# A decoder block on one core: one gather for both rows of an expert, and the low part of the up-projection's rows on GpSimd

## The chip, the cores and the metric

The kernel runs on one core of a Trainium2 chip. A core has a matrix engine (TensorE, PE in the profile; its weight loads are PEld), a vector engine (VectorE, DVE), a scalar engine (ScalarE, ACT), GpSimd (POOL) and a queue engine that issues DMAs (SyncE, SP). The on-chip memories are SBUF and PSUM; PE writes to PSUM, and DVE and ACT read and write both. The metric is the device time of one execution in microseconds (us).

## The reference, cut to what matters

The block has a mixer (attention and a short convolution), a layer norm, an expert layer and a second norm, for 1024 tokens of width 1024. All is float32. The expert layer has 16384 experts; each expert is one row `u` and one row `v` of 1024 numbers. A token picks 8 heads x 16 = 128 experts with gates `g`, and then:

```
u = jnp.take(u_experts, ec, axis=0)
a = jax.nn.gelu(jnp.einsum('tkd,td->tk', u, xc), approximate=False)
vv = jnp.take(v_experts, ec, axis=0)
return jnp.einsum('tk,tkd->td', gc * a, vv)
...
h = layer_norm(DN_ALPHA * h + ff, ln2_g[l], ln2_b[l])
```

## The kernel before

The 1024 tokens are eight blocks of 128. For four of them (`ROWS`, blocks 0, 1, 6 and 7) the expert layer is computed by **gathered rows**: for each of the 128 picks k, GpSimd gathers the picked row of `u` for all 128 tokens (an indirect DMA of 128 rows of 4 KB, line 148), DVE multiplies it by the token's `h1` and sums it into one number per token (line 150, the "up product"; a second small instruction reads the sum out). After 128 picks ACT applies gelu to all 128 x 128 numbers (line 152), DVE multiplies by the gates (line 153), and then for each pick GpSimd gathers the row of `v` (line 160) and DVE adds row times number to an accumulator in PSUM (line 162, the "down add"). That is 4 x 256 = 1024 operations on DVE and as many gathers. The rows stand in five buffers of 4 KB per partition (tag `t4k`); a gather waits until the operation five back has freed its buffer.

The other four blocks (2 to 5, 512 tokens) go through the **dense** layer: all 16384 experts in 128 chunks, on PE. `up(c)` loads chunk c of the transposed `u` table (`uraw`), splits it into a high part `uh` (a copy on ACT, line 120) and a low part `ul` (a subtraction, line 121), and multiplies both with the split `hT`, 24 matmuls. Then come the gelu `ge` on ACT, its product with the gates `gq` on DVE (line 690), and a split into `Wh` (ACT) and `Wl` (DVE). `down(q, jj)` does the same for four chunks' rows of `v`: `vh` on ACT, `vl` on GpSimd, 24 matmuls on the split W, and two adds of the result to `accT` on DVE (line 722). There are 128 such up units and 128 down units; `uh`, `ul`, `vh` and `vl` have two buffers each, the `W` parts five, and the raw loads four.

**Stage 1**, ahead of the dense stage, runs the mixer, the norm and the picking of experts for two blocks at a time; its last part builds the gates for the dense layer (`oh` and `ol` on DVE, 64 of each). The gathered operations are laid between its steps as soon as a block's picks are known (`step`, `advance_rows`), and further into the dense units by `advance(unit)`. The last part of the program (`finish`) transposes `accT`, adds `h1` and norms the four dense blocks.

The order of the instructions on each engine is set by a scheduler when the kernel is built; each engine runs its own in order.

Of the kernel before, what the change touches and what calls it, by code (L numbers as in the profile page):

```python
# [77 lines left out]
def block_kernel(ctx: ExitStack, tc: tile.TileContext, d, out):  # L78
# [47 lines left out]
    gp = ctx.enter_context(tc.tile_pool(name="gp", bufs=1, reuse_waits="tile"))  # L126
    pg = ctx.enter_context(tc.tile_pool(name="pg", bufs=1, space=PS, reuse_waits="tile"))

    def second_norm(tb, src):
        par = []  # L130
        for i in (2, 3):
            p = gp.tile([P, D], F32, name="ln2", tag="t4k", bufs=NGATHER)
            G.dma_start(p, ln2d[:, i:i + 1].to_broadcast([P, 1, D]).rearrange("p a e -> p (a e)"))
            par.append(p)
        o = gp.tile([P, D], F32, name="o", tag="t4k", bufs=NGATHER)
        layer_norm(o, src, par, gp)
        G.dma_start(out[tb * P:(tb + 1) * P], o)

    def gathered(tb):
        g = gw[tb].rearrange("p h k -> p (h k)")  # L140
        h1 = gp.tile([P, D], F32, name="h1", tag="t4k", bufs=NGATHER)
        G.dma_start(h1, h1d[tb])
        h1p = pg.tile([P, D], F32, name="pg")
        act(h1p, h1, AF.Copy)
# [9 lines left out]
        acc = pg.tile([P, D], F32, name="pg")
        h1 = gp.tile([P, D], F32, name="h1", tag="t4k", bufs=NGATHER)
        G.dma_start(h1, h1d[tb])
        act(acc, h1, AF.Copy, scale=ALPHA)
# [25 lines left out]
    with ExitStack() as s1:  # L183
# [196 lines left out]
        def rows_in(gi):  # L380

            blocks, nb, n, t0 = spans(gi)
            first = weights(0)
# [396 lines left out]
def lay_out(i):  # L780
    def m(name):
        return np.asarray(i[name])
# [32 lines left out]
```

## Time and profile before

| what | value |
|---|---|
| time, median of 3 runs | 2746.32 us (2743.99 to 2756.95) |
| the profiled execution, its time and its span | 2743.4 us, 2741.6 us |
| stage 1, up to the last of the gates | 0 to 1184 us |
| the dense stage, first to last matmul | 1230.66 to 2632 us |
| end of the dense stage to the end of the span | 110 us |

A row of a group of instructions names the line, the engine, the operation, the tile written, the tiles read and their shapes, and after x the count; behind the first bar stand the busy time in us and the mean of one in ns, behind the second the idle time of the engine just before them, with what ended it. The names `row` and `pg` in L150 and L162 are the gathered row and the block in PSUM; line numbers are those of the kernel before.

### The profile page before, as it was taken

The numbers are of one execution on the slowest core, as the hardware profiler recorded it, in microseconds if no ns is written. First come the engines' busy times: TensorE is split into PE (matmuls) and PEld (weight loads), VectorE is DVE, ScalarE is ACT, GpSimd is POOL, SyncE is SP. The second block draws the span as 40 slices with busy tenths as digits, with TensorE's granted clock in tenths as the row PEclk, the third lists the DMA queues.
The fourth block names the chain that finished last, engine by engine and source line by source line (L and its number), as shares of the span: only waits on it lengthen the run. The fifth ranks groups of instructions, "written<-read, shape, count | busy, mean of one in ns | idle before, by whom it ended". The sixth has DMA issues, their size and how long they took to land. (4 is left out here: it accounts for less than half of the span.)

```text
span 2741.6 us, 33269 instructions
## 1 busy us (share of the span) xinstructions
PE 2290.9 (84%) x11032; PEld 1917.8 (70%) x11032; DVE 2303.3 (84%) x4956; ACT 798.1 (29%) x1307; POOL 1415.2 (52%) x1233
## 2 busy tenths in 40 slices
PE   8999699789887622219999999999999999999940
PEld 7888587678766522218888888888888888888830
DVE  2158889999999999978888888888888888888897
ACT  2123122242443323224232322323232332323201
POOL 1000533443353344436667676666767666666753
PEclk9899799799977755559999999999999999999975
DMA  6355999899979788899999999999999999999987
GB/s 203 99 155 175 347 376 332 311 336 354 337 286 337 253 317 293 309 337 322 343 337 340 336 352 350 341 351 335 342 354 334 347 344 346 339 342 353 335 314 263
DMA packets 293900, 862.21 MB, mean 314 GB/s; under 512 B 25824, under 2 KB 97760, under 8 KB 289504
## 3 DMA queue, kind: packets, MB, share of 16 engines
q0 software_dynamic: 150480, 548.47, 54.5%
q1 hardware_dynamic: 143248, 311.62, 33.1%
q8 instruction: 87, 1.43, 0.2%
q14 instruction: 85, 0.70, 0.1%
HBM read 815.95 MB, written 44.04 MB: 314 GB/s over the span
## 5 line engine op out<-in xcount | busy, mean ns | idle before, releaser
L148 POOL DMA_INDIRECT row<-in_u,ix x512 | 532.9, 1041 | 586.7 <-DVE row L150 242.9
L160 POOL DMA_INDIRECT row<-in_v,ix x512 | 554.8, 1084 | 474.4 <-DVE pg L162 229.9
L162 DVE SCALAR_TENSOR_TENSOR pg<-row,a,pg 128x1024 f32<-128x1024 f32 x512 | 656.4, 1282 | 33.8 <-DMA row<-in_v,ix 27.8
L684 PE MATMUL pd<-hT,uh 128*128 128x512 f32 x2048 | 635.8, 390 | 42.8 <-ACT uh L120 42.8
L150 DVE SCALAR_TENSOR_TENSOR row<-row,pg 128x1024 f32<-128x1024 f32 x512 | 611.7, 1212 | 45.4 <-DMA row<-in_u,ix 44.8
L684 PEld LDWEIGHTS pd<-hT,uh 128*128 128x128 f32 x2048 | 385.4, 188 | 123.0 <-ACT uh L120 43.0
L716 PE MATMUL pd<-Wl,vh 128*128 128x512 f32 (+1 forms) x1056 | 402.3, 383 | 0.0
L684 PE MATMUL pd<-hT,ul 128*128 128x512 f32 x1024 | 399.3, 390 | 0.0
L716 PE MATMUL pd<-Wh,vh 128*128 128x512 f32 (+1 forms) x1056 | 397.4, 383 | 0.2 <-ACT Wh L120 0.2
L716 PE MATMUL pd<-Wh,vl 128*128 128x512 f32 (+1 forms) x1056 | 392.1, 383 | 0.3 <-POOL vl L121 0.3
L121 POOL TENSOR_TENSOR vl<-vraw,vh 128x1024 fp32r<-128x1024 f32 x128 | 309.4, 2417 | 72.7 <-ACT vh L120 68.6
L267 PE MATMUL pk<-o,oh 128*128 128x128 f16 x512 | 109.2, 277 | 208.2 <-DVE oh L261 131.3
L370 PE MATMUL mm<-x,raw 128*128 128x256 f32 x1152 | 269.2, 386 | 13.1 <-DMA x<-in_xT 7.7
L120 ACT ACTIVATE vh<-vraw 128x1024 fp32r<-128x1024 f32 x128 | 135.9, 1062 | 455.7 <-PE pd L716 302.1
L722 DVE TENSOR_TENSOR accT<-accT,pd 128x512 f32<-128x512 f32 (+1 forms) x256 | 169.4, 667 | 109.8 <-PE pd L716 97.8
L370 PEld LDWEIGHTS mm<-x,raw 128*128 128x128 f32 x1152 | 215.8, 193 | 45.2 <-issue 8.1
L370 PE MATMUL mm<-h,raw 128*128 128x256 f32 x1024 | 238.1, 385 | 1.5 <-ACT h L539 1.0
L716 PEld LDWEIGHTS pd<-Wh,vl 128*128 128x128 f32 x1056 | 198.4, 188 | 39.3 <-POOL vl L121 0.7
L716 PEld LDWEIGHTS pd<-Wl,vh 128*128 128x128 f32 x1056 | 198.5, 188 | 38.9 <-DVE Wl L121 0.2
L716 PEld LDWEIGHTS pd<-Wh,vh 128*128 128x128 f32 x1056 | 198.0, 188 | 39.2 <-ACT Wh L120 0.4
L121 DVE TENSOR_TENSOR ul<-uraw,uh 128x1024 fp32r<-128x1024 f32 x128 | 159.7, 1248 | 76.1 <-ACT uh L120 70.8
L684 PEld LDWEIGHTS pd<-hT,ul 128*128 128x128 f32 x1024 | 192.8, 188 | 40.9 <-DVE ul L121 0.8
(211 smaller groups left out, 2756.0 us busy)
## 6 DMA issues: line engine op xcount, KB each, us to landing
raw<-in_wall SPq DMA_DIRECT2D x168, 512.0 KB
uraw<-in_uT SPq DMA_DIRECT2D x128, 512.0 KB
vraw<-in_vL SPq DMA_DIRECT2D x128, 512.0 KB
gd<-st SPq DMA_DIRECT2D x32, 1024.0 KB
gq<-gd SPq DMA_DIRECT2D x32, 1024.0 KB
row<-in_u,ix POOLq DMA_INDIRECT x512
row<-in_v,ix POOLq DMA_INDIRECT x512
x<-in_xT SPq DMA_DIRECT2D x16, 256.0 KB
```

The lines of the kernel that those rows point to most:

```text
L120: act(dh, src, AF.Copy)
L121: eng.tensor_tensor(dl, src, dh.bitcast(F32), op=ALU.subtract)
L148: G.indirect_dma_start(out=row, out_offset=None, in_=d["u"], in_offset=bass.IndirectOffsetOnAxis(ap=idx[tb][:, k:k + 1], axis=0))
L150: V.scalar_tensor_tensor(row, row, 1.0, h1p, op0=ALU.mult, op1=ALU.mult, accum_out=a[:, k:k + 1])
L160: G.indirect_dma_start(out=row, out_offset=None, in_=d["v"], in_offset=bass.IndirectOffsetOnAxis(ap=idx[tb][:, k:k + 1], axis=0))
L162: V.scalar_tensor_tensor(acc, row, a[:, k:k + 1], acc, op0=ALU.mult, op1=ALU.add)
L267: nc.tensor.matmul(ps[:, t], oh[:, :, t2 + t], o1[:, t2 + t], start=True, stop=False)
L370: nc.tensor.matmul(ps[:, :n], w[:, j], mov[:, j, :n], start=(j == 0), stop=(j == NJ - 1))
L684: nc.tensor.matmul(ps, w[:, j], hT[z][:, j], start=(j == 0 and k == 0), stop=(j == NJ - 1 and k == 2))
L716: nc.tensor.matmul(ps, vv[:, j % 2, k], w[:, t0:t0 + n], start=(k == 0 and p == 0), stop=(k == QUAD - 1 and p == 2))
L722: V.tensor_tensor(o, o, ps, op=ALU.add)
```

## The change

The two expert tables become one, `uv`, whose row holds `u` and `v` of an expert, 8 KB. One gather per pick brings both (512 gathers instead of 1024), into five buffers of 8 KB (tag `uv`). The up product of pick k is now followed, for that pick alone, by gelu and by the product with the gate, two ACT instructions on 128 x 1 numbers, and the down add of pick k-1 stands behind the up product of pick k. `h1` lies in SBUF instead of PSUM, and the accumulator holds the one PSUM tile from the start. In `up`, the subtraction that makes `ul` goes to GpSimd. The tag `T` of stage 1 has three buffers instead of four, and the ring of the gathers' descriptors is set to 8192 bytes. Line numbers of the changed kernel: gather 153, up product 156, gelu 157, gate 158, down add 161, subtraction 122.

```
+SCRATCH = 8192
...
+    def pair(name):
+        return gp.tile([P, 2, D], F32, name=name, tag="uv", bufs=NGATHER)
+
     def second_norm(tb, src):
...
+        par = pair("ln2")
+        G.dma_start(par, ln2d[:, 2:4].to_broadcast([P, 2, D]))
+        o = pair("o")[:, 0]
+        layer_norm(o, src, (par[:, 0], par[:, 1]), gp)
         G.dma_start(out[tb * P:(tb + 1) * P], o)
 
     def gathered(tb):
...
         g = gw[tb].rearrange("p h k -> p (h k)")
-        h1 = gp.tile([P, D], F32, name="h1", tag="t4k", bufs=NGATHER)
+        h1 = gp.tile([P, D], F32, name="h1")
         G.dma_start(h1, h1d[tb])
-        h1p = pg.tile([P, D], F32, name="pg")
-        act(h1p, h1, AF.Copy)
+        acc = pg.tile([P, D], F32, name="pg")
+        act(acc, h1, AF.Copy, scale=ALPHA)
         a = gp.tile([P, P], F32, name="a", bufs=2)
-        for k in range(P):
-            row = gp.tile([P, D], F32, name="row", tag="t4k", bufs=NGATHER)
-            G.indirect_dma_start(out=row, out_offset=None, in_=d["u"],
-                                 in_offset=bass.IndirectOffsetOnAxis(ap=idx[tb][:, k:k + 1], axis=0))
-            V.scalar_tensor_tensor(row, row, 1.0, h1p, op0=ALU.mult, op1=ALU.mult, accum_out=a[:, k:k + 1])
-            yield True
-        act(a, a, AF.Gelu)
-        V.tensor_tensor(a, a, g, op=ALU.mult)
...
-        for k in range(P):
-            row = gp.tile([P, D], F32, name="row", tag="t4k", bufs=NGATHER)
-            G.indirect_dma_start(out=row, out_offset=None, in_=d["v"],
-                                 in_offset=bass.IndirectOffsetOnAxis(ap=idx[tb][:, k:k + 1], axis=0))
-            V.scalar_tensor_tensor(acc, row, a[:, k:k + 1], acc, op0=ALU.mult, op1=ALU.add)
-            yield True
+        rows = {}
+        for k in range(P + 1):
+            if k < P:
+                rows[k] = pair("row")
+                G.indirect_dma_start(out=rows[k].rearrange("p a e -> p (a e)"), out_offset=None, in_=d["uv"],
+                                     in_offset=bass.IndirectOffsetOnAxis(ap=idx[tb][:, k:k + 1], axis=0))
+                ru = rows[k][:, 0]
+                V.scalar_tensor_tensor(ru, ru, 1.0, h1, op0=ALU.mult, op1=ALU.mult, accum_out=a[:, k:k + 1])
+                act(a[:, k:k + 1], a[:, k:k + 1], AF.Gelu)
+                act(a[:, k:k + 1], a[:, k:k + 1], AF.Copy, scale=g[:, k:k + 1])
+                yield True
+            if k:
+                V.scalar_tensor_tensor(acc, rows.pop(k - 1)[:, 1], a[:, k - 1:k], acc, op0=ALU.mult, op1=ALU.add)
+                yield True
         second_norm(tb, acc)
...
-            split(uh, ul, raw)
+            split(uh, ul, raw, G)
...
+        "uv": f(np.concatenate([m("u_experts")[0], m("v_experts")[0]], axis=1)),
```

The scheduler makes a new order from this. Counted down DVE's order, this many gathered operations (up products and down adds) stand ahead of four places:

| place in DVE's order | before | after |
|---|---|---|
| the 64th and last `ol` of the gates | 370 (242 up, 128 down) | 414 (208 up, 206 down) |
| the split of `hT`, ahead of the first dense matmul | 382 | 429 |
| the 128th `ge` product | 959 | 1015 |
| the 253rd of the 256 `accT` adds | 966 | 1024 |

ACT's order has 59 loads of an activation table instead of 21, 54 instead of 16 of them ahead of the first `uh`.

POOL's order in the middle of the dense stage, about the 85th `vl`, before (`row<-in_u` is a gather of up rows; x after a row is a count):

```order
L148 DMA row<-in_u,ix_9615 128x1024 x13
L121 TENSOR_TENSOR vl<-vraw,vh 128x1024 x2
L148 DMA row<-in_u,ix_9615 128x1024 x5
L121 TENSOR_TENSOR vl<-vraw,vh 128x1024
L148 DMA row<-in_u,ix_9615 128x1024
```

The same place after (`row<-in_uv` is a gather of pairs):

```order
L153 DMA row<-in_uv,ix_9611 128x2048 x4
L122 TENSOR_TENSOR ul<-uraw,uh 128x1024
L122 TENSOR_TENSOR vl<-vraw,vh 128x1024 x2
L153 DMA row<-in_uv,ix_9611 128x2048
L122 TENSOR_TENSOR ul<-uraw,uh 128x1024
L153 DMA row<-in_uv,ix_9611 128x2048 x4
L122 TENSOR_TENSOR ul<-uraw,uh 128x1024
L122 TENSOR_TENSOR vl<-vraw,vh 128x1024
L122 TENSOR_TENSOR ul<-uraw,uh 128x1024
L122 TENSOR_TENSOR vl<-vraw,vh 128x1024
```

Half of the gathers are gone from the queue, and a `ul` stands there for each `vl`; for four chunks there are now about nine gathers, four `ul` and four `vl`.

DVE's order in the dense stage, at a run of up units, before:

```order
L121 TENSOR_TENSOR Wl<-ge,Wh 128x512
L162 SCALAR_TENSOR_TENSOR pg<-row,a,pg 128x1024
L121 TENSOR_TENSOR ul<-uraw,uh 128x1024
L162 SCALAR_TENSOR_TENSOR pg<-row,a,pg 128x1024
L690 TENSOR_TENSOR ge<-ge,gq 128x512
```

And after:

```order
L689 TENSOR_TENSOR ge<-ge,gq 128x512
L161 SCALAR_TENSOR_TENSOR pg<-row,a,pg 128x1024
L122 TENSOR_TENSOR Wl<-ge,Wh 128x512
L156 SCALAR_TENSOR_TENSOR row,a<-row,h_12215 128x1024
L689 TENSOR_TENSOR ge<-ge,gq 128x512
L161 SCALAR_TENSOR_TENSOR pg<-row,a,pg 128x1024
```

`ul` has left this engine, and up products (L156) and down adds (L161) of one block now take turns, where before a block had all its up products first.

The last rows of DVE's dense stage, before:

```order
L162 SCALAR_TENSOR_TENSOR pg<-row,a,pg 128x1024
L722 TENSOR_TENSOR accT<-accT,pd 128x256
L162 SCALAR_TENSOR_TENSOR pg<-row,a,pg 128x1024 x55
L105 TENSOR_REDUCE lnst<-sums 128x1
L106 TENSOR_SCALAR lnst<-lnst 128x1
```

And after:

```order
L161 SCALAR_TENSOR_TENSOR pg<-row,a,pg 128x1024
L721 TENSOR_TENSOR accT<-accT,pd 128x256 x2
L106 TENSOR_REDUCE lnst<-sums 128x1
L107 TENSOR_SCALAR lnst<-lnst 128x1 x2
L721 TENSOR_TENSOR accT<-accT,pd 128x256
```

The 55 down adds that stood behind the last `accT` add are gone from this place; the last down add now stands ahead of the last four `accT` adds.

## Rows read from the trace of the kernel before

**Rows 1.** The page's head and its busy time, share of the span, instructions.

```profile
span 2741.6 us, 33269 instructions
...
PE 2290.9 (84%) x11032; PEld 1917.8 (70%) x11032; DVE 2303.3 (84%) x4956; ACT 798.1 (29%) x1307; POOL 1415.2 (52%) x1233
```

**Rows 2.** Windows: length; busy us of PE, PEld, DVE, ACT, POOL; PEclk; DMA share; GB/s.

```profile
200.00:1184.00 984.00, 699.64 (x3836) 591.26 (x3834) 931.66 (x2990) 301.47 (x623) 396.90 (x380) 0.79 0.86 309
1184.00:1231.00 47.00, 2.32 (x16) 1.97 (x17) 29.56 (x55) 9.91 (x12) 16.62 (x18) 0.50 1.03 377
1231.00:2632.00 1401.00, 1400.47 (x6268) 1162.58 (x6268) 1192.27 (x1508) 432.01 (x539) 945.17 (x721) 1.00 0.95 341
2632.00:2742.00 110.00, 0.65 (x6) 0.41 (x4) 89.59 (x112) 9.47 (x18) 49.02 (x54) 0.52 0.81 293
```

**Rows 3.** Groups of DVE, last 110 us: count, busy, mean ns, idle before.

```profile
L162 DVE SCALAR_TENSOR_TENSOR pg<-row,a,pg 128x1024 f32<-128x1024 f32 x55 | 70.9, 1289 | 12.8 <-DMA row<-in_v,ix 11.1 <-DVE pg L162 0.4
```

**Rows 4.** Waits of PE in the dense stage: total, times, longest.

```profile
PE pd L684 <- ACT uh L120: 42.8, 1, 42.8
PE pd L716 <- POOL vl L121: 0.3, 1, 0.3
```

**Rows 5.** Groups of DVE by line in stage 1 (200 to 1184 us).

```profile
L150 DVE SCALAR_TENSOR_TENSOR row<-row,pg 128x1024 f32<-128x1024 f32 x242 | 289.5, 1209 | 29.1 <-DMA row<-in_u,ix 28.7 <-issue 0.2
L162 DVE SCALAR_TENSOR_TENSOR pg<-row,a,pg 128x1024 f32<-128x1024 f32 x128 | 163.1, 1274 | 1.6 <-DMA row<-in_v,ix 1.5
...
L116 DVE SCALAR_TENSOR_TENSOR r<-r,lnst,ln 128x1024 f32<-128x1024 f32 x6 | 7.6, 1274 | 0.0
```

**Rows 6.** Groups of ACT in stage 1: table loads and a 128x1 activation.

```profile
L109 ACT ACT_TABLE_LOAD x4 | 5.1, 1283 | 0.1
...
L109 ACT ACTIVATE lnst<-lnst 128x1 f32<-128x1 f32 x7 | 1.3, 201 | 2.0 <-DVE lnst L108 2.0
```

**Rows 7.** Groups of DVE by line in the dense stage (1231 to 2632 us).

```profile
L162 DVE SCALAR_TENSOR_TENSOR pg<-row,a,pg 128x1024 f32<-128x1024 f32 x328 | 421.1, 1284 | 18.8 <-DMA row<-in_v,ix 15.1 <-DVE accT L722 0.7 <-issue 0.2
L150 DVE SCALAR_TENSOR_TENSOR row<-row,pg 128x1024 f32<-128x1024 f32 x256 | 305.3, 1215 | 9.3 <-DMA row<-in_u,ix 9.2
L722 DVE TENSOR_TENSOR accT<-accT,pd 128x512 f32<-128x512 f32 x240 | 163.3, 685 | 109.5 <-PE pd L716 97.6 <-issue 11.3
L121 DVE TENSOR_TENSOR ul<-uraw,uh 128x1024 fp32r<-128x1024 f32 x128 | 159.7, 1248 | 76.1 <-ACT uh L120 70.8 <-issue 3.0 <-PE pd L684 1.8
L121 DVE TENSOR_TENSOR Wl<-ge,Wh 128x512 fp32r<-128x512 f32 x128 | 92.5, 723 | 0.7 <-ACT Wh L120 0.7
L690 DVE TENSOR_TENSOR ge<-ge,gq 128x512 f32<-128x512 f32 x128 | 92.0, 718 | 0.8 <-ACT ge L689 0.8
```

**Rows 8.** Groups of POOL by line in the dense stage.

```profile
L160 POOL DMA_INDIRECT row<-in_v,ix x327 | 353.7, 1082 | 227.7 <-DVE pg L162 164.0 <-issue 37.9 <-PE pd L716 13.0
L121 POOL TENSOR_TENSOR vl<-vraw,vh 128x1024 fp32r<-128x1024 f32 x128 | 309.4, 2417 | 72.7 <-ACT vh L120 68.6 <-issue 2.7
L148 POOL DMA_INDIRECT row<-in_u,ix x256 | 277.0, 1082 | 156.2 <-DVE row L150 105.1 <-issue 32.0 <-PE pd L716 5.3
```

**Rows 9.** Timeline at 1266 us, DVE: start, length, operation.

```profile
1265.14 1.22 DVE L121 TENSOR_TENSOR ul<-uraw,uh 128x1024 fp32r<-128x1024 f32 x1
...
1268.07 3.27 DVE L121 TENSOR_TENSOR ul<-uraw,uh 128x1024 fp32r<-128x1024 f32 x1
```

**Rows 10.** The same stretch on POOL.

```profile
1267.86 2.40 POOL L121 TENSOR_TENSOR vl<-vraw,vh 128x1024 fp32r<-128x1024 f32 x1 [1.83 <-ACT vh L120]
```

**Rows 11.** Timeline at 1575 us, DVE: an up product.

```profile
1576.53 1.22 DVE L150 SCALAR_TENSOR_TENSOR row<-row,pg 128x1024 f32<-128x1024 f32 x1 [0.63 <-DMA row<-in_u,ix]
```

**Rows 12.** The same stretch on POOL.

```profile
1575.16 2.41 POOL L121 TENSOR_TENSOR vl<-vraw,vh 128x1024 fp32r<-128x1024 f32 x1
```

**Rows 13.** Waits of ACT in the dense stage.

```profile
ACT vh L120 <- PE pd L716: 302.1, 91, 6.6
```

**Rows 14.** Waits of POOL's gathers of down rows in the dense stage.

```profile
POOL row L160 <- DVE pg L162: 164.0, 150, 13.1
```

More of the change, by code (lines that the diff above doesn't have):

```diff
@@ L127, in block_kernel @@
     pg = ctx.enter_context(tc.tile_pool(name="pg", bufs=1, space=PS, reuse_waits="tile"))
+    def pair(name):
+        return gp.tile([P, 2, D], F32, name=name, tag="uv", bufs=NGATHER)
     def second_norm(tb, src):
[L130 to L136, printed above, removed]
+        par = pair("ln2")
+        G.dma_start(par, ln2d[:, 2:4].to_broadcast([P, 2, D]))
+        o = pair("o")[:, 0]
+        layer_norm(o, src, (par[:, 0], par[:, 1]), gp)
         G.dma_start(out[tb * P:(tb + 1) * P], o)
@@ L140, in gathered @@
         g = gw[tb].rearrange("p h k -> p (h k)")
-        h1 = gp.tile([P, D], F32, name="h1", tag="t4k", bufs=NGATHER)
+        h1 = gp.tile([P, D], F32, name="h1")
         G.dma_start(h1, h1d[tb])
-        h1p = pg.tile([P, D], F32, name="pg")
-        act(h1p, h1, AF.Copy)
+        acc = pg.tile([P, D], F32, name="pg")
+        act(acc, h1, AF.Copy, scale=ALPHA)
         a = gp.tile([P, P], F32, name="a", bufs=2)
-        for k in range(P):
-            row = gp.tile([P, D], F32, name="row", tag="t4k", bufs=NGATHER)
-            G.indirect_dma_start(out=row, out_offset=None, in_=d["u"],
-                                 in_offset=bass.IndirectOffsetOnAxis(ap=idx[tb][:, k:k + 1], axis=0))
-            V.scalar_tensor_tensor(row, row, 1.0, h1p, op0=ALU.mult, op1=ALU.mult, accum_out=a[:, k:k + 1])
-            yield True
-        act(a, a, AF.Gelu)
-        V.tensor_tensor(a, a, g, op=ALU.mult)
[L154 to L157, printed above, removed]
-        for k in range(P):
-            row = gp.tile([P, D], F32, name="row", tag="t4k", bufs=NGATHER)
-            G.indirect_dma_start(out=row, out_offset=None, in_=d["v"],
-                                 in_offset=bass.IndirectOffsetOnAxis(ap=idx[tb][:, k:k + 1], axis=0))
-            V.scalar_tensor_tensor(acc, row, a[:, k:k + 1], acc, op0=ALU.mult, op1=ALU.add)
-            yield True
+        rows = {}
[12 more added lines that the diff above has]
+                yield True
         second_norm(tb, acc)
@@ L383, in rows_in @@
             first = weights(0)
-            x = p2.tile([P, NJ, NM], F32, name="x", tag="T", bufs=4)
+            x = p2.tile([P, NJ, NM], F32, name="x", tag="T", bufs=3)
             for j in range(0, NJ, 2):
@@ L530, in normed @@
             blocks, nb, n, t0 = spans(gi)
-            h_ = p2.tile([P, NJ, NM], F32, name="h", tag="T", bufs=4)
+            h_ = p2.tile([P, NJ, NM], F32, name="h", tag="T", bufs=3)
             for b, tb in enumerate(blocks):
@@ L639, in block_kernel @@
             x, qkv = xin
-            y = p2.tile([P, NJ, NM], F32, name="y", tag="T", bufs=4)
+            y = p2.tile([P, NJ, NM], F32, name="y", tag="T", bufs=3)
             for b in range(2):
@@ L769, in block_kernel @@
         for i in (2, 3):
-            p = gp.tile([P, D], F32, name="ln2", tag="t4k", bufs=NGATHER)
+            p = pair("ln2")[:, 0]
             nc.sync.dma_start(p, ln2d[:, i:i + 1].to_broadcast([P, 1, D]).rearrange("p a e -> p (a e)"))
@@ L797, in lay_out @@
         "skT": f(np.stack([m("sub_keys1")[0].T, m("sub_keys2")[0].T])),
-        "u": f(m("u_experts")[0]),
-        "v": f(m("v_experts")[0]),
+        "uv": f(np.concatenate([m("u_experts")[0], m("v_experts")[0]], axis=1)),
         "uT": f(m("u_experts")[0].reshape(NC, P, NJ, P).transpose(0, 3, 2, 1)),
@@ L805 @@
 def kernel(**inputs):
-    nc = bacc.Bacc("TRN2", target_bir_lowering=False, num_devices=1)
+    nc = bacc.Bacc("TRN2", target_bir_lowering=False, num_devices=1, dynamic_dma_scratch_size=SCRATCH)
     arrays = {f"in_{k}": a for k, a in lay_out(inputs).items()}
```

## The prediction, on record before the result

> **What bounds the kernel now.** I read the page's head first: VectorE (DVE) is busy 84% of the span, and so is TensorE (PE) [rows 1]. A mean over the span hides that they are busy in different stages, so the windows by stage come next [rows 2]. In stage 1 (200 to 1184 us) DVE works 931.66 of 984 us and PE 699.64: DVE is the bound. In the dense stage (1231 to 2632) PE works 1400.47 of 1401 us at a granted clock of 1.00, and DVE 1192.27: PE is the bound, and the waits of PE there show 0.3 us on `vl`, with 42.8 us on the first `uh` just ahead of the stage [rows 4]. The last 110 us have almost no PE (0.65 us): DVE finishes 55 down adds, 70.9 us of work and 12.8 us of gaps [rows 3], and then the last norms. So a microsecond of DVE counts in full in stage 1 and in the tail. In the dense stage it counts only beyond what DVE has spare: 1401 - 1192 = 209 us.
>
> **The change, part by part.**
>
> *Tail.* Counted down DVE's order, all 1024 gathered operations now stand ahead of the 253rd `accT` add; before, 55 stood behind all of them. The tail loses that row [rows 3]: 70.9 + 12.8 = 84 us. The norms behind it (110 - 84 = 26 us) stay. Both ends of this term lie close: **-84**, unless the dense stage itself ends later, which is the third term.
>
> *Stage 1.* At the last `ol` of the gates, 414 gathered operations have run instead of 370 (208 products and 206 adds, for 242 and 128). The two rows of stage 1 give (289.5 + 163.1) / 370 = 1.22 us each [rows 5], so 44 more are 54 us on the engine that bounds the stage. Credit: DVE's 28.7 + 1.5 us on gathers [rows 5]; five buffers now hold ten operations' rows instead of five, so some of this goes. Bounds 0 and 30; I take 15, half, because the bytes for each operation are the same and the DMA share was 0.86 [rows 2]. Debit: the order has 54 activation table loads ahead of the first `uh` instead of 16, each 1.283 us [rows 6]: 49 us of ACT, whose idle time in the stage is 984 - 301 = 683 us [rows 2]. A down add waits for its scalar, which takes two 128x1 activations at 0.2 us and perhaps one load, 1.7 us [rows 6]; an add and a product stand between (1.27 + 1.21 us [rows 5]), so most is covered. Bounds 0 and 49, taken as 11, nearer to the covered end. Sum 54 - 15 + 11 = **+50**, ends 54 - 30 = +24 and 54 + 49 = +103. This work isn't new: it is what left the dense stage and the tail, done earlier where it is paid in full.
>
> *Dense stage, bare need of DVE.* The 128 `ul` subtractions leave DVE: -160 us [rows 7]. It has 595 gathered operations instead of 584 (1024 - 429, against 256 + 328): +14. The up product now reads `h1` from SBUF instead of PSUM; the nearest row for such an operation with two SBUF inputs is the norm's at 1274 ns [rows 5], against 1215 [rows 7]: 297 x 0.06 = +18. So 1192 - 160 + 14 + 18 = 1064 us of 1401. This looks like ample room.
>
> *Dense stage, GpSimd.* POOL now makes `ul` and `vl`: 256 subtractions at 2417 ns [rows 8], 619 us, and 297 gathers. If an 8 KB gather costs what a 4 KB one costs (1082 ns [rows 8]) that is 321 us, together 940, as before (945 [rows 2]); if issue goes with bytes, 642, together 1261. Both fit in 1401; I take the first, because an instruction still names 128 rows.
>
> *What the two do to each other.* A row decides here. At 1268.07 DVE's `ul`, two SBUF inputs, took 3.27 us; the one before took 1.22 [rows 9]. POOL's `vl` ran from 1267.86 to 1270.26 [rows 10], and `ul` ended 1.08 us after it: it stood still until POOL was done. An up product of before that started inside a `vl` took its plain 1.22 us [rows 11, 12]: one operand lay in PSUM. The Trainium skill says the same in SBUF — State Buffer, "Who interferes with whom": a VectorE instruction with two SBUF inputs and a GpSimd instruction that reads SBUF share a read interface, the one that starts first keeps it for the whole instruction and the other blocks; by that rule this change puts more of both kinds against each other, and the rows above agree with it.
>
> The operations that can collide rise from 384 (`ul`, `ge`, `Wl`) against 128 `vl` to 553 (297 products, 128 `ge`, 128 `Wl`) against 256. Their price:
> - low: `ul`, `ge` and `Wl` of before lie only some 0.035 us over their plain times in the mean (`ul` 1248 ns against 1.22 us) [rows 7, 9], about 14 us in all, where chance would have given 384 x (309/1401) x 1.21 = 102 us, since `vl` falls into the down units and those operations into the up units. With the same seventh, the new cost is 0.14 x 295 = 41 us.
> - by chance: 553 starts x (619/1401) x half of 2.42 us = 295 us.
> - high: an up product and a down add alternate, so a subtraction that starts within an add (1.28 us [rows 7]) meets the product behind it: 256 x (2.42 - 0.64) = 455 us.
>
> I take 350: the products now run in every unit, so the phases that kept `vl` apart don't protect them, and a subtraction can start only when DVE is in an add or idle. To this come waits that stay: DMA 15.1 + 9.2 us [rows 7], and scalars that sit on ACT behind a `vh` that waits for PE: 302.1 us in 91 waits, 3.3 us each [rows 13]; an add has about that much cover, so I count five of them, 16 us, an estimate. DVE's need is 1064 + 350 + 40 = 1454 of 1401 us: **+53**. Ends: 0 (1064 + 41 + 40 = 1145) and 1064 + 455 + 40 - 1401 = +158. What is late next is `ge`, then `Wh` and `Wl`, then PE, which so far waited for nothing.
>
> *Free edits.* The three `T` buffers, the smaller ring and the paired `ln2` load: SP's order hardly moves and no row shows a wait on them; 0.
>
> **Sum** against the profiled execution (2743.4 us, 2.9 below the median of 2746.3): 2743.4 + 50 - 84 + 53 = 2762.4, in terms of the median **2765 us**.
>
> **Rivals.**
> 1. *The stages stay as they are, and the tail is won.* The low price holds, DVE has 250 us to spare, X = 0: 2746.3 + 50 - 84 = 2712 us. For it: PE waited for nothing in 1401 us [rows 4], and the collisions of before were few. Against it: rows 9 and 10 and the alternation. It decides as long as the lock costs less than about 317 us (X below 20). This ends on the other side.
> 2. *No change.* The lock costs 317 to 345 us, X is 20 to 48, and what left the tail comes back in stage 1 and as small waits of PE: about 2746.
> 3. *POOL's queue holds PE up.* `ul` now stands on POOL behind runs of four gathers, each of which waits until an add has freed a buffer; the gathers of down rows waited 164.0 us on DVE in 150 waits, up to 13.1 [rows 14]. If each of 128 `ul` comes late by such a wait's mean, 1.1 us, that is 140 us on PE instead of 53: 2746 + 50 - 84 + 140 = 2852. Against it: `vl` stood in the same queue and cost PE 0.3 us. A gather that costs twice as much would push the same way.
>
> **How the numbers follow.** About half a per cent (14 us) is what a measurement of this kernel can tell from no change. Chances: the forecast 0.37, rival 1 0.35, rival 2 0.18, rival 3 0.10. The forecast by itself reaches from 2760 (X = 48) to 2820. Faster takes rival 1, same takes rival 2 with the fringe of the forecast, slower the rest: 0.35, 0.20, 0.45. The range reaches over most of rival 1 (with stage 1 at its low end, +24, that one would come to 2686) and to rival 3: 2695 to 2850.
>
> **What would show it.** Right: up products over 1.5 us in the mean in the dense stage, with the long ones ending 1.2 us after a `vl` or `ul`; DVE near full there; PE waiting for `Wh`, `Wl` or `ul` some tens of us; first dense matmul some 50 us later; end about 26 us behind PE's last. Wrong: products at 1.27 us all through (no lock for this form), PE still waiting for under 5 us, or a stage 1 that ends at 1231 or far beyond 1330 because ACT's table loads stand in the chain of scalars.

## The result, and the profile after

The changed kernel takes 2874.72 us (median of 4 runs, 2872.19 to 2877.56) against 2746.07: a ratio of 1.0465 with a 95% interval of 1.0443 to 1.0487, slower by 129 us. Its profiled execution took 2872.19 us, with a span of 2870.4. The windows by stage, with the bounds of the changed kernel (columns as in [rows 2]):

```profile
200.00:1250.00 1050.00, 708.36 (x3831) 593.27 (x3830) 982.41 (x2991) 433.39 (x1076) 279.60 (x214) 0.78 0.82 313
1250.00:1306.50 56.50, 1.93 (x15) 1.57 (x15) 39.80 (x64) 11.59 (x29) 21.24 (x13) 0.50 1.02 385
1306.50:2849.00 1542.50, 1450.01 (x6272) 1172.05 (x6272) 1422.34 (x1426) 550.42 (x1132) 1050.59 (x552) 0.98 0.86 309
2849.00:2870.40 21.40, 0.00 (x0) 0.00 (x0) 16.59 (x49) 4.53 (x11) 0.59 (x1) 0.59 0.31 123
```

The first dense matmul starts at 1306.8 us instead of 1230.7, the last one ends at 2848.9 instead of 2632.7. Stage 1 and what lies up to the dense stage became 76.1 us longer, the dense stage 140.1 (1542.1 for 1402.0), and the tail 87.4 shorter (21.5 for 108.9): 76.1 + 140.1 - 87.4 = 128.8, the difference of the two spans.

In the dense stage DVE is now busy 1422 of 1542 us, where it was 1192 of 1402, though 128 subtractions have left it. The groups of DVE in this stage, against [rows 7]:

```profile
L156 DVE SCALAR_TENSOR_TENSOR row<-row,h 128x1024 f32<-128x1024 f32 x293 | 528.9, 1805 | 1.1 <-DMA row<-in_uv,ix 1.1
L161 DVE SCALAR_TENSOR_TENSOR pg<-row,a,pg 128x1024 f32<-128x1024 f32 x294 | 378.1, 1286 | 76.8 <-ACT a L158 76.5
L689 DVE TENSOR_TENSOR ge<-ge,gq 128x512 f32<-128x512 f32 x128 | 205.2, 1603 | 25.5 <-ACT ge L688 24.1
L122 DVE TENSOR_TENSOR Wl<-ge,Wh 128x512 fp32r<-128x512 f32 x128 | 195.6, 1528 | 8.8 <-ACT Wh L121 8.7
```

The down add (L161) keeps its 1.28 us. The up product has gone from 1215 to 1805 ns, `ge` from 718 to 1603 and `Wl` from 723 to 1528. These are the three that read two SBUF operands. Their excess is 293 x 0.590 + 128 x 0.885 + 128 x 0.805 = 173 + 113 + 103 = 389 us. The groups of POOL, against [rows 8]:

```profile
L153 POOL DMA_INDIRECT row<-in_uv,ix x289 | 413.6, 1431 | 366.3 <-DVE pg L161 330.5 <-issue 17.2 <-PE pd L715 6.4
L122 POOL TENSOR_TENSOR ul<-uraw,uh 128x1024 fp32r<-128x1024 f32 x128 | 320.2, 2502 | 55.1 <-ACT uh L121 40.9 <-ACT a L157 12.4 <-PE pd L715 0.7
L122 POOL TENSOR_TENSOR vl<-vraw,vh 128x1024 fp32r<-128x1024 f32 x128 | 316.7, 2476 | 55.8 <-ACT vh L121 51.5 <-ACT a L157 3.1
```

And PE, which waited for nothing before [rows 4], waits in the dense stage (start left out; total, times, longest):

```profile
PE pd L715 <- POOL vl L122: 25.9, 27, 2.5
PE pd L715 <- ACT Wh L121: 25.1, 11, 4.6
PE pd L683 <- POOL ul L122: 18.7, 16, 2.6
PE pd L715 <- DVE Wl L122: 12.3, 15, 2.4
```

All its waits there sum to 91 us. PE's busy time rose as well, from 1401 to 1450 us, with the same matmuls and a mean granted clock of 0.98: 91 + 49 = 140, the whole of the dense stage's loss. One place shows how it comes about. The timeline of DVE:

```profile
2665.36 7.21 DVE L689 TENSOR_TENSOR ge<-ge,gq 128x512 f32<-128x512 f32 x1 [1.20 <-ACT ge L688]
2673.27 0.69 DVE L122 TENSOR_TENSOR Wl<-ge,Wh 128x512 fp32r<-128x512 f32 x1 [0.69 <-ACT Wh L121]
...
2760.87 2.88 DVE L689 TENSOR_TENSOR ge<-ge,gq 128x512 f32<-128x512 f32 x1
```

and of POOL in the same two stretches:

```profile
2665.00 2.40 POOL L122 TENSOR_TENSOR vl<-vraw,vh 128x1024 fp32r<-128x1024 f32 x1
2667.35 2.37 POOL L122 TENSOR_TENSOR ul<-uraw,uh 128x1024 fp32r<-128x1024 f32 x1
2669.69 2.33 POOL L122 TENSOR_TENSOR vl<-vraw,vh 128x1024 fp32r<-128x1024 f32 x1
...
2760.66 2.55 POOL L122 TENSOR_TENSOR ul<-uraw,uh 128x1024 fp32r<-128x1024 f32 x1
2763.17 2.86 POOL L122 TENSOR_TENSOR vl<-vraw,vh 128x1024 fp32r<-128x1024 f32 x1
```

One `ge`, plain 0.7 us, took 7.21 us: it began 0.36 us after a `vl`, POOL ran `vl`, `ul` and `vl` with no gap, to 2672.02, and `ge` ended 0.55 us after the last of them. Here DVE wasn't let in between GpSimd instructions that follow each other at once. That isn't a rule: at 2760.87 another `ge` began under a `ul` with a `vl` right behind it, and it ended at 2763.75, 0.54 us after the `ul`, while that `vl` took 2.86 us instead of 2.4. Of 59 DVE operations of this stage that began in this way, 28 were kept out through the second subtraction as well, and 31 came in ahead of it. What decides which isn't shown. Behind the `ge` of 7.21 us stood `Wh` on ACT, and PE waited 4.41 us for it:

```profile
2673.29 0.79 PE L715 MATMUL pd<-Wh,vh 128*128 128x512 f32 x1 [4.41 <-ACT Wh L121]
```

The windows around this wait show what PE lost besides:

```profile
2668.70:2673.30 4.60, 0.19 (x2) 0.02 (x1) 3.90 (x2) 0.63 (x1) 3.32 (x2) 0.84 0.84 319
2673.30:2678.80 5.50, 5.50 (x13) 4.06 (x14) 4.90 (x8) 1.65 (x5) 1.15 (x1) 0.51 0.04 15
2678.80:2690.00 11.20, 11.20 (x51) 9.29 (x50) 10.60 (x14) 3.64 (x10) 6.83 (x4) 1.00 0.97 341
```

PE was almost idle for 4.6 us, and for 5.5 us behind the wait the granted clock was 0.51, the lower level of 1.2 GHz. PE was busy all through these 5.5 us but ran only 13 matmuls, one in 0.42 us; the next 11.2 us, at 1.00, have 51, one in 0.22. A wait of this kind costs twice, but not every wait is of this kind: past its start the dense stage has some 76 waits and twelve stretches at the lower level. These add up to 51 us, with PE busy for 46 of them, so they cost some 23 us, about half of the 49. The other half isn't the clock's. A part of it, by an estimate, is the last matmul ahead of each wait, whose row is 0.39 us long where in a run the next one starts after 0.22: 76 x 0.17 = 13 us. The rest stays open.

### The profile page after: what moved, and what is told of

It is laid out like the page before. It is cut to its first block, busy times and chain, and to the rows that moved or that the text cites. A ratio compares the mean times of both kernels' runs of the same rounds, so it can differ in the third digit from the quotient of the medians.

```text
span 2870.4 us, 32954 instructions
## 1 busy us (share of the span) xinstructions
PE 2348.5 (82%) x11032; PEld 1928.9 (67%) x11032; DVE 2521.4 (88%) x4824; ACT 1045.5 (36%) x2361; POOL 1359.5 (47%) x841
## 5 line engine op out<-in xcount | busy, mean ns | idle before, releaser
L153 POOL DMA_INDIRECT row<-in_uv,ix x512 | 712.8, 1392 | 1173.2 <-DVE pg L161 627.1
L156 DVE SCALAR_TENSOR_TENSOR row<-row,h 128x1024 f32<-128x1024 f32 x512 | 794.0, 1551 | 19.6 <-DMA row<-in_uv,ix 19.5
L161 DVE SCALAR_TENSOR_TENSOR pg<-row,a,pg 128x1024 f32<-128x1024 f32 x512 | 656.6, 1283 | 88.0 <-ACT a L158 87.2
L157 ACT ACTIVATE a<-a 128x1 f32<-128x1 f32 x512 | 103.8, 203 | 1079.8 <-DVE row L156 1079.2
L715 PE MATMUL pd<-Wh,vh 128*128 128x512 f32 (+1 forms) x1056 | 408.5, 390 | 32.1 <-ACT Wh L121 25.1
L683 PE MATMUL pd<-hT,ul 128*128 128x512 f32 x1024 | 405.9, 396 | 19.0 <-POOL ul L122 18.7
L715 PE MATMUL pd<-Wl,vh 128*128 128x512 f32 (+1 forms) x1056 | 410.8, 390 | 12.4 <-DVE Wl L122 12.3
L122 POOL TENSOR_TENSOR ul<-uraw,uh 128x1024 fp32r<-128x1024 f32 x128 | 320.2, 2502 | 55.1 <-ACT uh L121 40.9
L122 POOL TENSOR_TENSOR vl<-vraw,vh 128x1024 fp32r<-128x1024 f32 x128 | 316.7, 2476 | 55.8 <-ACT vh L121 51.5
L689 DVE TENSOR_TENSOR ge<-ge,gq 128x512 f32<-128x512 f32 x128 | 205.2, 1603 | 25.5 <-ACT ge L688 24.1
L369 PEld LDWEIGHTS mm<-h,raw 128*128 128x128 f32 x1024 | 193.0, 194 | 32.1 <-ACT cT L557 5.6
```

What stands on the lines that cost most here:

```text
L153: G.indirect_dma_start(out=rows[k].rearrange("p a e -> p (a e)"), out_offset=None, in_=d["uv"], in_offset=bass.IndirectOffsetOnAxis(ap=idx ...
L156: V.scalar_tensor_tensor(ru, ru, 1.0, h1, op0=ALU.mult, op1=ALU.mult, accum_out=a[:, k:k + 1])
L157: act(a[:, k:k + 1], a[:, k:k + 1], AF.Gelu)
L161: V.scalar_tensor_tensor(acc, rows.pop(k - 1)[:, 1], a[:, k - 1:k], acc, op0=ALU.mult, op1=ALU.add)
L369: nc.tensor.matmul(ps[:, :n], w[:, j], mov[:, j, :n], start=(j == 0), stop=(j == NJ - 1))
L683: nc.tensor.matmul(ps, w[:, j], hT[z][:, j], start=(j == 0 and k == 0), stop=(j == NJ - 1 and k == 2))
```

## The experiments

The theory: GpSimd's subtractions and DVE's operations with two SBUF operands shut each other out, and that makes the dense stage slow. The rivals: the chain of each pick (gather, product, gelu, gate, add) or POOL's fuller queue does it by itself. "Loss" below is the excess of DVE's operations with two SBUF operands over their plain times (1215 ns for 128x1024, 718 and 723 for `ge` and `Wl`, the means of the kernel before, which hold its own few collisions), from the groups of the dense stage; the dense stage is first to last matmul. The verdicts stand on the ratio to the kernel before with its 95% interval.

| kernel | subtractions on GpSimd | loss, us | first dense matmul | dense stage | tail | median us | ratio |
|---|---|---|---|---|---|---|---|
| before | `vl` | 4 | 1230.7 | 1402 | 109 | 2746 | |
| changed | `ul`, `vl` | 389 | 1306.8 | 1542 | 21 | 2874.7 | 1.0465 [1.0443, 1.0487] |
| e1 | `ul`, `vl` | 269 | 1233.0 | 1503 | 106 | 2847.0 | 1.0374 [1.0356, 1.0391] |
| e2 | `vl` | 194 | 1307.3 | 1431 | 22 | 2762.7 | 1.0066 [1.0049, 1.0083] |
| e3 | `ul`, `vl` | 315 | 1220.9 | 1576 | 64 | 2860.3 | 1.0416 [1.0399, 1.0434] |
| e4 | `ul`, `vl` | 263 | 1309.0 | 1458 | 22 | 2786.8 | 1.0147 [1.0130, 1.0164] |
| e5 | `ul`, `vl` | 0 | 1226.4 | 1418 | 67 | 2707.6 | 0.9858 [0.9842, 0.9875] |
| e6 | `ul`, `vl` | 0 | 1236.1 | 1408 | 105 | 2749.9 | 1.0010 [0.9997, 1.0023] |
| e9 | `ul`, `vl` | 0 | 1264.6 | 1406 | 84 | 2758.2 | 1.0045 [1.0033, 1.0057] |

**e1: `ul` on GpSimd alone**, in the kernel before.

```
-            split(uh, ul, raw)
+            split(uh, ul, raw, G)
```

> The kernel before with one edit: the ul subtraction on GpSimd. Rows are still gathered one table at a time and the up product still reads h1 from PSUM. Lock theory (a GpSimd subtraction and a DVE operation with two SBUF operands shut each other out): products stay at 1.21 us; only ge and Wl collide, which in the changed kernel cost (1603 - 680) x 128 + (1528 - 680) x 128 = 226 us of DVE; DVE needs 1192 - 160 + 226 = 1258 of 1401 us, so the dense stage stays at 1400 to 1420 us and some of the tail's 84 us go: 2670 to 2750. Queue theory (ul late on POOL behind gathers): PE waits 20 to 140 us on ul: 2765 to 2890.

It was 2847.02 us, where the lock theory had 2750 at most. The half of the change that frees DVE loses 101 us by itself. The window of the dense stage (columns as in [rows 2]) and DVE's groups:

```profile
1233.00:2736.00 1503.00, 1432.22 (x6271) 1170.24 (x6272) 1304.39 (x1379) 429.77 (x539) 1226.17 (x850) 0.99 0.91 318
...
L150 DVE SCALAR_TENSOR_TENSOR row<-row,pg 128x1024 f32<-128x1024 f32 x256 | 306.1, 1212 | 82.8 <-DMA row<-in_u,ix 82.6
L121 DVE TENSOR_TENSOR Wl<-ge,Wh 128x512 fp32r<-128x512 f32 x128 | 257.3, 2010 | 19.2 <-ACT Wh L120 16.8
L690 DVE TENSOR_TENSOR ge<-ge,gq 128x512 f32<-128x512 f32 x128 | 196.5, 1535 | 21.0 <-ACT ge L689 20.9
```

The product, with one operand in PSUM, is untouched at 1212 ns; `Wl` and `ge` pay. DVE was busy only 1304 of 1503 us, so it wasn't short of time in the mean; PE waits all the same:

```profile
PE pd L684 <- POOL ul L121: 38.9, 23, 4.0
PE pd L716 <- POOL vl L121: 28.3, 22, 3.2
```

In its size this looked like the queue theory, 67 us on POOL and 31 us of busy time more on PE (1432 for 1401). e6 decides what lies behind it.

**e2: the pairs alone**, the changed kernel with `ul` back on DVE.

```
-            split(uh, ul, raw, G)
+            split(uh, ul, raw)
```

> The changed kernel with the ul subtraction back on DVE; the pair gathers and the chain of gelu and gate for each pick stay. Lock theory: only the 128 vl collide with the products, so products fall from 1805 to about 1450 ns in the dense stage and ge and Wl to under 800; DVE needs about 1023 + 160 + 100 = 1283 us, the dense stage takes 1401 to 1450, and with stage 1 at +76 and the tail at -88 the time is 2735 to 2785. Chain theory (DVE waits on ACT for each pick's scalar, and the gathers on the adds, whatever the lock does): DVE's waits on ACT stay at 75 us or more and the dense stage over 1500: 2830 or more.

2762.70 us: within what the lock theory gave, +17 on the kernel before. The two halves, +101 and +17, come near the +129 of both. Half as many subtractions on GpSimd cost half as much (194 us), now in four kinds of operation; `ge` and `Wl` stood further from their plain times than expected:

```profile
L156 DVE SCALAR_TENSOR_TENSOR row<-row,h 128x1024 f32<-128x1024 f32 x293 | 421.7, 1441 | 0.0
...
L122 DVE TENSOR_TENSOR ul<-uraw,uh 128x1024 fp32r<-128x1024 f32 x128 | 223.9, 1750 | 35.9 <-ACT uh L121 35.7
...
L689 DVE TENSOR_TENSOR ge<-ge,gq 128x512 f32<-128x512 f32 x128 | 138.5, 1082 | 0.4 <-ACT ge L688 0.4
L122 DVE TENSOR_TENSOR Wl<-ge,Wh 128x512 fp32r<-128x512 f32 x128 | 105.1, 821 | 0.9 <-ACT Wh L121 0.9
```

**e3: no lock for the product.** It multiplies with the accumulator, which lies in PSUM.

```
-                V.scalar_tensor_tensor(ru, ru, 1.0, h1, op0=ALU.mult, op1=ALU.mult, accum_out=a[:, k:k + 1])
+                V.scalar_tensor_tensor(ru, ru, 1.0, acc, op0=ALU.mult, op1=ALU.mult, accum_out=a[:, k:k + 1])
```

> The changed kernel, but the up product multiplies the row with the accumulator in PSUM instead of h1 in SBUF, so that it has one SBUF operand (it computes another number than the reference's). Lock theory: products at 1.21 us, 173 us less of DVE's time in the dense stage; the 256 subtractions still collide with ge and Wl: DVE needs 1249 us and its waits, the dense stage falls from 1542 to 1405 to 1450: 2735 to 2785. Chain theory: products at 1.21 us too, but the dense stage stays over 1500: 2830 or more.

2860.26 us: the lock theory's number missed by 75 us or more. The products were at their plain time, but the loss didn't go with them; `ge` and `Wl` took it over, 885 to 1248 and 805 to 1216 ns each above plain:

```profile
L156 DVE SCALAR_TENSOR_TENSOR row<-row,pg 128x1024 f32<-128x1024 f32 x298 | 360.7, 1210 | 1.3 <-DMA row<-in_uv,ix 0.4
L689 DVE TENSOR_TENSOR ge<-ge,gq 128x512 f32<-128x512 f32 x128 | 251.7, 1966 | 53.3 <-ACT ge L688 52.7
L122 DVE TENSOR_TENSOR Wl<-ge,Wh 128x512 fp32r<-128x512 f32 x128 | 248.1, 1939 | 32.4 <-ACT Wh L121 31.5
```

The dense stage was 1576 us, longer than the changed kernel's though the loss is smaller (315 for 389), so the loss alone doesn't set its length. PE's busy time was 1474 us there, at a mean granted clock of 0.95, and its longest waits were for `vh` on ACT, 53.7 us. The order differs too: 375 gathered operations ahead of the last of the gates, 31 behind the last `accT` add, so this run alone doesn't separate the theories. e5, with the same counts, does.

**e4: no lock for `ge` and `Wl`.** Gelu and the product with the gates stay in the PSUM tile.

```
-            ge = dn.tile([P, TD], F32, name="ge", bufs=2)
-            act(ge, ps, AF.Gelu)
-            V.tensor_tensor(ge.rearrange("p (a t) -> p a t", t=TG), ge.rearrange("p (a t) -> p a t", t=TG),
+            act(ps, ps, AF.Gelu)
+            V.tensor_tensor(ps.rearrange("p (a t) -> p a t", t=TG), ps.rearrange("p (a t) -> p a t", t=TG),
...
-            split(wh, wl, ge)
+            split(wh, wl, ps)
```

> The changed kernel, but gelu and the product with the gates stay in the PSUM tile of the matmul, so that ge and Wl have one SBUF operand each. Lock theory: ge and Wl near 0.7 us, 226 us less of DVE's time, of which the products take back up to 100 (they meet more of the subtractions): dense stage 1405 to 1470, 2735 to 2800. Chain theory: over 1500, 2830 or more. A third way: the matmul's PSUM tiles are held longer and PE waits for them.

2786.79 us, with the counts of the changed kernel's order unchanged (414 and 1024): 88 us of its 129 are gone. The product went the other way, from 1805 to 2113 ns:

```profile
L156 DVE SCALAR_TENSOR_TENSOR row<-row,h 128x1024 f32<-128x1024 f32 x293 | 618.9, 2113 | 2.0 <-DMA row<-in_uv,ix 2.0
...
L688 DVE TENSOR_TENSOR pd<-pd,gq 128x512 f32<-128x512 f32 x128 | 88.9, 694 | 44.4 <-ACT pd L687 42.4
L122 DVE TENSOR_TENSOR Wl<-pd,Wh 128x512 fp32r<-128x512 f32 x128 | 87.4, 683 | 7.8 <-ACT Wh L121 7.6
```

**e5: both edits.** No operation of the dense units on DVE reads two SBUF operands.

> The changed kernel with both edits of the two runs before it: the up product multiplies with the accumulator in PSUM (another number than the reference's), and gelu and the gate product stay in PSUM. No DVE operation of the dense units reads two SBUF operands, while GpSimd still makes ul and vl and the gathers and the chain of each pick stay. Lock theory: products 1.21, ge and Wl 0.7 us, no more waits of PE than some 10 us, dense stage 1401 to 1420 us: 2680 to 2750. Chain and queue theory: waits of DVE on ACT and of PE on ul and vl stay, the dense stage over 1480: 2800 or more.

2707.64 us. Against e3, with the same counts in the order, only `ge` and `Wl` differ; the time falls by 153 us and the dense stage from 1576 to 1418:

```profile
L156 DVE SCALAR_TENSOR_TENSOR row<-row,pg 128x1024 f32<-128x1024 f32 x298 | 361.4, 1213 | 0.9
...
L688 DVE TENSOR_TENSOR pd<-pd,gq 128x512 f32<-128x512 f32 x128 | 89.2, 697 | 133.3 <-ACT pd L687 133.0
L122 DVE TENSOR_TENSOR Wl<-pd,Wh 128x512 fp32r<-128x512 f32 x128 | 87.9, 687 | 39.0 <-ACT Wh L121 38.8
```

```profile
PE pd L714 <- DVE Wl L122: 2.4, 1, 2.4
PE pd L683 <- POOL ul L122: 1.7, 1, 1.7
...
PE pd L714 <- POOL vl L122: 0.2, 1, 0.2
```

GpSimd still made both low parts and the chain of each pick was still there. By themselves the chain and the queue don't cause the dense stage's loss. The gathers of pairs are also back at their plain time, 947 ns, for which the changed kernel had 1431:

```profile
L153 POOL DMA_INDIRECT row<-in_uv,ix x298 | 282.1, 947 | 346.2 <-DVE pg L161 284.7 <-issue 21.0 <-DMA vraw<-in_vL 5.4
```

**e6: e1 with the gate in PSUM**, so single gathers, `ul` and `vl` on GpSimd.

> The kernel before with ul on GpSimd, and gelu and the gate product left in PSUM. Lock theory: the 280 us that ge and Wl lost with ul on GpSimd alone are gone, PE no longer waits on ul and vl, the dense stage is back at 1401 to 1420 and DVE has room for some of the tail's adds: 2660 to 2755. Queue theory (POOL with ul, vl and twice as many gathers is too full, 1226 of 1503 us): PE still waits 40 us or more on ul and vl, DVE over 100 us on gathers: 2800 or more.

2749.87 us. POOL was as full as in e1 (1177 of 1408 us), and PE hardly waited:

```profile
PE pd L684 <- POOL ul L121: 1.8, 2, 1.4
PE pd L715 <- POOL vl L121: 1.2, 2, 0.8
```

So the waits on `ul` and `vl` in e1 were the way the loss reached PE, not its source. Nothing was gained on the kernel before either: 53 down adds still stand behind the last matmul in this order.

**e7: the kernel before with the gate in PSUM.**

> The kernel before with one edit: gelu and the gate product stay in PSUM. Its collisions cost only some 14 us of DVE, which has 209 us to spare: no change by the lock theory, 2738 to 2752. If holding the PSUM tiles longer costs PE something, slower, and then the other runs with this edit carry that cost too.

2745.25 us, ratio 0.9997 [0.9986, 1.0008]: no change. The edit costs nothing by itself.

**e8: the pairs with `ul` on DVE and the gate in PSUM.**

> The changed kernel with ul back on DVE, and gelu and the gate product in PSUM. Lock theory: ge and Wl give back 69 us, products and ul take some of it; DVE needs about 1310 us with 30 us of waits, the dense stage falls from 1431 to 1405 to 1425: 2735 to 2757. Chain theory: as with ul back on DVE alone, 2763.

2743.94 us, ratio 0.9990 [0.9981, 1.0000]: no change that can be told, 19 us less than e2. The dense stage was 1411 us.

**e9: e5 with the reference's numbers.** `h1` is copied to PSUM for the last two gathered blocks, whose two banks are taken from the matmuls' six.

```
+        if late:
+            h1p = late[0].tile([P, D], F32, name="h1p")
+            act(h1p, h1, AF.Copy)
+            h1 = h1p
...
-        pd = s2.enter_context(tc.tile_pool(name="pd", bufs=6, space=PS, reuse_waits="tile"))
+        pd = s2.enter_context(tc.tile_pool(name="pd", bufs=4, space=PS, reuse_waits="tile"))
+        late.append(s2.enter_context(tc.tile_pool(name="ph", bufs=1, space=PS, reuse_waits="tile")))
```

> The changed kernel, ul and vl on GpSimd, with gelu and the gate product in PSUM and, for the last two gathered blocks, h1 copied to PSUM for the up products (two banks taken from the matmuls' six). It computes the reference. Lock theory: hardly a collision in the dense stage, products near 1.25 us, waits of PE under 10 us, dense stage 1401 to 1425; its order has 366 gathered operations ahead of the last of the gates and 43 behind the last accT add, so stage 1 ends where it did before (first dense matmul 1220 to 1240) and the tail is 22 + 43 x 1.25 = 76 us: 2700 to 2735. If four banks are too few for the matmuls, PE waits and it is 2750 or more.

2758.18 us: the dense stage was as expected, but stage 1 wasn't. The windows:

```profile
1264.60:2670.30 1405.70, 1401.74 (x6272) 1162.94 (x6272) 1048.50 (x1428) 550.70 (x1131) 893.75 (x557) 1.00 0.93 342
2670.30:2754.00 83.70, 0.15 (x2) 0.00 (x0) 69.64 (x121) 19.91 (x60) 16.98 (x19) 0.52 0.73 276
```

The dense stage is back at 1406 us with both low parts on GpSimd. The first dense matmul came at 1264.6, 34 us after that of the kernel before, with as many gathered operations done (381 for 382 in the order). The pairs cost something in stage 1 that isn't the moved work.

**e15: `vl` on DVE, `ul` on GpSimd.**

```
-            split(vh, vl, raw, G)
+            split(vh, vl, raw)
```

> The changed kernel with ul on GpSimd and vl on DVE, the reverse of the run with ul on DVE alone, which had 128 vl on GpSimd and lost 204 us of DVE to them (1.6 us each). If the price is per GpSimd subtraction and not a matter of its phase: again 180 to 220 us lost, 2755 to 2780. If ul is the worse one because it runs in the up units beside ge and Wl: over 240 us lost, mostly in ge and Wl, and 2790 or more.

2782.03 us, ratio 1.0127 [1.0111, 1.0143], 19 us more than e2, and between the two expectations. The loss is 194 us, as in e2:

```profile
L156 DVE SCALAR_TENSOR_TENSOR row<-row,h 128x1024 f32<-128x1024 f32 x293 | 383.1, 1308 | 0.0
...
L122 DVE TENSOR_TENSOR vl<-vraw,vh 128x1024 fp32r<-128x1024 f32 x128 | 233.3, 1828 | 5.6 <-ACT vh L121 5.6
...
L689 DVE TENSOR_TENSOR ge<-ge,gq 128x512 f32<-128x512 f32 x128 | 156.2, 1220 | 26.7 <-ACT ge L688 25.4
L122 DVE TENSOR_TENSOR Wl<-ge,Wh 128x512 fp32r<-128x512 f32 x128 | 117.0, 914 | 3.2 <-ACT Wh L121 3.0
```

27 + 78 + 64 + 24 us: with 128 subtractions on GpSimd the loss is the same, whichever of the two they make. The dense stage was 20 us longer than in e2, and PE waited 26.6 us on `vl`, which came from DVE now; that the same loss hurts more there is seen, its reason isn't shown.

**e10 and e13: e9 with more gathered operations early.** One constant, `EARLY`, is (4, 2) in e10 and (4, 4) in e13 instead of (3, 1).

> The kernel without collisions (products and gate in PSUM) with one constant changed, so that its order has 401 gathered operations ahead of the last of the gates instead of 366, and 9 behind the last accT add instead of 43. If stage 1 and the tail both go at DVE's pace and trade one for one, 35 x 1.22 = 43 us later into the dense stage (first dense matmul near 1307) and 34 x 1.25 = 42 us off the tail: the same time, 2750 to 2766. If stage 1 has room for them, 2715 to 2740.

> The kernel without collisions with the constant at (4, 4), after (4, 2) took 11 us off the kernel before: 403 gathered operations ahead of the last of the gates, 1019 ahead of the last accT add. If the tail's rest can still be put into stage 1's idle time: 2720 to 2735. If stage 1 is full by now: 2735 to 2745.

2735.34 us, ratio 0.9956 [0.9943, 0.9969], and 2734.68, ratio 0.9955 [0.9940, 0.9971]. Stage 1 did have room: in e10 35 more operations, 43 us of DVE, delayed the first dense matmul by 16 us (1280.6), while the tail fell to 38 us. In e10 44 products that still read `h1` from SBUF fell into the dense stage and took 2023 ns each, and the stage was 1417 us: the lock again. Both kernels compute the reference and beat the kernel before, by 0.4%.

**e11: e9 without gelu's table loads.** The gelu of each pick is a plain copy.

> The kernel without collisions, with the gelu of each pick replaced by a plain copy (other numbers than the reference's), so that ACT's order has 11 table loads ahead of the first uh instead of 53; the same 366, 381 and 981 gathered operations stand at the three places. That kernel's first dense matmul was at 1264.6 us against 1230.7 of the kernel before, with about as many gathered operations done. If the table loads between gelu and the exponentials hold stage 1 up: first dense matmul 1225 to 1245, time 2720 to 2740. If not (the pairs, or the order): 1258 or later, 2750 or more.

2747.32 us, 11 us less than e9, with the first dense matmul at 1259.3, 5 us earlier: the table loads are some 5 to 11 of the 34 us. One profiled execution doesn't tell it closer: the kernels with the stage 1 of before (before, e1, e6, e7) had their first dense matmul at 1230.7 to 1236.1.

**e12: e9 without both ACT instructions of a pick.**

> The kernel without collisions, with both ACT instructions of each pick left out, so that the down add takes the product's sum as it is (other numbers than the reference's). Its order has 378, 396 and 996 gathered operations at the three places instead of 366, 381 and 981. If the small ACT instructions, which wait in ACT's order for a DVE product, hold up stage 1: its 12 to 15 more operations are done no later, first dense matmul 1230 to 1255 (for 1264.6) and 2715 to 2740. If they don't: 1264.6 + 15 x 1.22 = 1283 and no gain in the sum, 2750 or more.

2733.42 us, ratio 0.9949 [0.9933, 0.9966]. The first dense matmul came at 1266.3, between the two expectations, with 396 instead of 381 operations done. If the 15 operations had cost DVE's pace, 15 x 1.22 = 18 us, the small ACT instructions, table loads among them, would account for some 17 of the 34 us; at the rate of e10, 16 us for 35 operations, the 15 would have cost 7 us, and it is some 5. How much of the 34 us is theirs stays open; the order differs in more than the counts.

## Why the prediction was wrong, by its own steps

**The tail, -84:** it measured -87. Right.

**Stage 1, +50 with ends at +24 and +103:** +66 at the last `ol` and +76 at the first dense matmul. The moved work was right: DVE's busy time rose by 51 us for 54 forecast [rows 2]. The gathered operations of stage 1 after, against [rows 5]:

```profile
L161 DVE SCALAR_TENSOR_TENSOR pg<-row,a,pg 128x1024 f32<-128x1024 f32 x206 | 263.1, 1277 | 9.4 <-ACT a L158 9.0 <-issue 0.2
L156 DVE SCALAR_TENSOR_TENSOR row<-row,h 128x1024 f32<-128x1024 f32 x208 | 251.7, 1212 | 15.8 <-DMA row<-in_uv,ix 15.7
```

DVE's waits on gathers fell from 30 to 16 us, as the credit said, but other waits came in their place, and the idle time rose from 52 to 68 us. The 10 us between stage 1 and the first matmul had no term; DVE's busy time there rose by as much, 39.8 us for 29.6 [rows 2], and ACT waited 13.7 us there for the first `uraw`, 10.6 before.

**The mechanism in the dense stage** was right: two SBUF operands against GpSimd, found in [rows 9, 10]. e5, e6 and e9 show it as the cause: without such pairs the stage takes 1406 to 1418 us, with both low parts on GpSimd. The rule named from the Trainium skill (SBUF — State Buffer, "Who interferes with whom") agrees in what collides: down adds and products with an operand in PSUM were at their plain time in all kernels. It gives one instruction as the time of a block; the row of 7.21 us shows a block through three, the one of 2.88 us a block through one.

**The price of the lock, 350 us:** 389, near it. The low price, scaled from the collisions of before, had nothing to say about this kernel, and "by chance" (295) was too low too. The price came to 1.5 us for each GpSimd subtraction in the changed kernel (389/256), e2 and e15 (194/128), and to 1.0 to 1.2 in e1, e3 and e4, where a part of the operations was taken out of the lock and the rest paid for them. It isn't a constant of the subtraction: the kernel before has 128 `vl` on GpSimd too, and its three kinds of operations with two SBUF operands lost 4 us to them [rows 7]. With the products reading SBUF in every unit, the same 128 `vl` cost 194 us in e2, and `ul`, `ge` and `Wl` paid two thirds of it. Why they hardly met before was argued in the prediction (phases of the units), and no run shows it.

**The plain time of the up product from SBUF:** 1212 ns in stage 1, no more than from PSUM; the +18 us weren't there.

**The step that failed** is the way from DVE's need to PE's loss, +53 with +158 as its end; it measured +140. The sum took PE's loss as what DVE needs beyond 1401 us: bare need 1064, lock 350 and waits 40. DVE's busy time was near its terms, 1422 us (lock 389, the rest 1033), which is 21 us beyond 1401. But DVE was also idle for 120 us instead of 40, of which 76.5 were adds waiting for their scalar from ACT, for which the sum had 16: the waits are the term that was mis-sized, and DVE, ACT, POOL and PE did not overlap as it supposed. Seen from PE, the same 140 us are 91 us of waits and 49 us more of busy time, some 23 of them at the lower granted clock; for these the sum had no term at all. e1 shows why a sum of needs doesn't do: there DVE had 199 us idle and PE lost 101, most of it in waits for `ul` and `vl`. In one such place a gather stood 2.15 us in POOL's queue until DVE freed its buffer (at 1600.41 us); then `ul` and `vl` ran behind it without a gap, a `ge` took 5.34 us under them, and PE waited 3.21 us for that `vl`. So one engine's delay is handed to the next, while each has time to spare in the mean. The range ended at 2850 because the terms' high ends weren't added up: 2746 + 103 - 84 + 158 = 2923 was the working's own end.

**Rival 3** (POOL's queue) saw the right symptom, PE waiting on `ul` and `vl`, 45 us, and its 2852 us is the nearest of the numbers, by luck: e6 shows that the queue doesn't do it without the lock.

## What to carry to other kernels

Before work goes from VectorE to GpSimd, list the VectorE operations that read two SBUF operands in the same stretch, and count a loss of 1 to 1.5 us for each 2.4 us GpSimd operation where the two kinds meet in every unit (1.0 to 1.5 in six kernels here; where they hardly met, in the kernel before, it was next to nothing). Freeing only some of the VectorE operations hands most of the loss to the others. Putting one operand of each into PSUM takes it away. And where a full TensorE gets short waits, read the granted clock behind them: what it loses there comes on top of the waits.

## What the runs showed of the hardware

Back-to-back instructions of GpSimd kept a VectorE operation out for all of their run, 7.21 us against 0.7; in other places of the same trace it came in behind the first, and then the second GpSimd instruction was the longer one (2.86 us for 2.4). GpSimd's gathers suffer from the same operations: 1431 ns each in the changed kernel, 1082 before [rows 8], 947 in e5, where hardly any VectorE operation had two SBUF operands. A gather of 8 KB rows costs GpSimd no more than one of 4 KB rows (947 ns in e5, 948 in e6). And behind a wait of 4.4 us PE ran for 5.5 us at a granted clock of 0.51, with a matmul every 0.42 us instead of every 0.22.
